# A list-scheduled decoder trunk: the planner's two rules outside the mix stage only, MLP blocks split from the residual stream, remainders of the output product by the vector engine

## The chip, the core and the metric

The kernel runs on one core of one Trainium2 chip. The metric is the time of one execution on the device in microseconds (us). Five engines take part, each with a queue of its own: TensorE (PE, the matmuls), VectorE (DVE), ScalarE (ACT), GpSimd (POOL) and SyncE (SP, which issues the loads).

## The reference

Two layers over a residual stream h of 512 tokens by 1024 channels in float32. Each layer is three steps:

```python
h = h + W_out [ attention_heads || mlstm_heads ](RMSNorm(h) @ W_in)
h = h + relu(RMSNorm(h) @ W1)^2 @ W2
h = h + sigmoid(RMSNorm(h) @ Wg + bg) * (p[i] @ Wp)
```

The attention has 8 heads of 64, two key heads, partial rotary positions, and reads for each query 128 keys that an indexer selects (the 128 largest scores). The mLSTM has 4 heads of 128, a causal convolution of width 4 ahead of its queries and keys, a forget and an input gate, and is stabilised by running maxima. W1 widens to 4096.

## The kernel before

h is held in the chip's memory, transposed, as eight blocks h[0] to h[7] of 128 channels by 512 tokens; the names const_1 to const_8 in rows below are these blocks. Each product is made of three matmuls in a reduced format: an operand x is split into hi, its rounded copy, and lo, the remainder x - hi, and hi*hi, hi*lo and lo*hi are added up (`mm3`). So for each weight tile of 128 x 1024, SP loads raw (three buffers), ACT copies it to hi, and lo is made in one of two ways, in `weight` (around line 527): DVE subtracts hi from raw; or, with adder=True, ACT writes the negated hi into lo and a DMA that POOL issues adds raw to it (an "adder"). Activation blocks are split the same way.

The three steps of a layer l are stages 3l (mix), 3l + 1 (MLP) and 3l + 2 (the gated step). The mix makes queries, keys, gates and the attention and mLSTM heads; `out_half` (line 1172) then multiplies the heads' outputs by W_OUT, four weight tiles in each of two halves, and DVE adds each block of the product to h. The MLP begins with `prep` (line 567): for each of the eight blocks it applies the norm's gain, splits the result into hi and lo, and adds up the squares for the norm's root, a running sum on POOL. With forms (the MLP's call) it also makes, for each pair of blocks, `right_sums` (line 749): half-width differences of the two, and their hi and lo, which a later product with summed weights reads. `split_block` (line 562) splits from h with the gain inside; `split` (line 744) splits a block that has the gain already.

The order of all instructions is worked out ahead by the class `Plan` (line 127). All operations of the kernel are recorded first, each with a label. `Plan.schedule` then runs through time with a table of costs: of the operations that are ready, each engine takes the most urgent by its label's priority, and the order found is written out for each engine. `lag` is what the plan allows for between an operation and the one that depends on it, 110 ns between two of VectorE. Lines 348 to 353 make an exception for small tiles: rooms "tiny" (128 x 4 and the like) and "wide" (128 x 32). `HOP` (200 ns) is the time after which the plan takes a buffer for free once its last reader is done; after an adder it takes `ADD` (5500 ns). Lines 361 to 364 hold that rule. These are numbers for the planning alone; on the chip, semaphores hold an instruction until what it needs is there. Operations of the label "forms" come behind those of "prep" in priority. Since every instruction is issued from line 395, all rows of the profile carry L395, and the tiles' names tell them apart.

Of the kernel before, what the change touches and what calls it, by code (L numbers as in the profile page):

```python
# [43 lines left out]
W_CQ, W_UP, W_QK, W_V, W_O, W_OUT, W_FF1, W_FF2, W_PLE, W_GATE, NW = 0, 2, 4, 12, 16, 20, 28, 60, 92, 94, 102  # L44
# [82 lines left out]
class Plan:  # L127
# [122 lines left out]
    def schedule(self):  # L250
# [15 lines left out]
        events, now, done = [], 0.0, 0  # L266
# [27 lines left out]
        while done < len(ops):  # L294
            moved, relaxed = True, False
            while moved or not (events or relaxed):
                relaxed = not moved
                moved = False
                for e in self.ENGINES:
                    if busy[e]:  # L300
                        continue
                    best = None
                    for key, q in queues[e].items():
                        while q and ops[q[0][1]].start is not None:
                            heapq.heappop(q)
                        if q and (best is None or q[0] < best[0]):
                            op = ops[q[0][1]]
                            if fits(op, relaxed):
                                best = (q[0], q)
                    if best is None:  # L310
                        continue
                    op = ops[heapq.heappop(best[1])[1]]
                    op.form = next(f for f in op.forms if f[0] == e)
                    op.start = op.begin = now
                    for b in op.new:
                        live[b.name] = (b, op.label, round(now / 1000))
                        if b.room in free:
                            b.place = free[b.room].pop(0)
                        for group, (kinds, cap) in self.caps.items():
                            if b.kind in kinds:  # L320
                                held[group] += 1
                    busy[e] = True
                    order.append(op)
                    op.end = now + self.cost(op.form)
                    if e == "sync" and not now:
                        op.end += 900.0
                    if e == "tensor":
                        if now - idle[0] > 3300.0:
                            idle[1] = now + 3600.0
                        if now < idle[1]:  # L330
                            op.end += self.cost(op.form)
                        idle[0] = op.end
                    heapq.heappush(events, (op.end, 0, op.n, e))
                    moved = True
                    if relaxed:
                        break
            if not events:
                stuck = [(o.n, o.label, [b.kind for b in o.new]) for e in self.ENGINES for q in queues[e].values()
                         for _, i in q[:3] for o in (ops[i],) if o.start is None]
                self.live = live  # L340
                self.stuck = []
                raise RuntimeError(f"no place: {done} of {len(ops)} {stuck[:20]} { {k: len(v) for k, v in free.items()} } {held}")
            now, what, n, e = heapq.heappop(events)
            op = ops[n]
            if what == 0:
                busy[e] = False
                done += 1
                for b in op.before:
                    o = ops[b]
                    wait = self.lag(self.source(op), o.forms[0][0])  # L350
                    if e == o.forms[0][0] == "vector" and o.writes[0].buf.room in ("tiny", "wide"):

                        wait = 0.0
                    o.ready = max(o.ready, now + wait)
                    o.left -= 1
                    if not o.left:
                        if o.ready <= now:
                            push(o)
                        else:
                            heapq.heappush(events, (o.ready, 1, o.n, None))  # L360
                for b in {id(v.buf): v.buf for v in op.reads + op.writes}.values():
                    b.users -= 1
                    if not b.users:
                        heapq.heappush(events, (now + (self.ADD if self.source(op) == "adder" else self.HOP), 2, n, b.name))
                        self.gone[b.name] = b
            elif what == 1:
                push(op)
            else:
                b = self.gone.pop(e)
                live.pop(b.name)  # L370
                if b.room in free:
                    free[b.room].append(b.place)
                for group, (kinds, cap) in self.caps.items():
                    if b.kind in kinds:
                        held[group] -= 1
# [31 lines left out]
class Trunk:  # L407
# [159 lines left out]
    def prep(self, l, gcol, forms=None):  # L567


        nc = self.nc  # L570
        label = nc.label
        cf = self.cf[l][0]
        xs, acc, last = [], None, None
        for k in range(KD):
            nc.label, nc.bias = ("prep", 0) if nc.stage else ("start", -STEP * k)
            hi, lo = self.slot([128, S], F32R), self.slot([128, S], F32R)
            if forms is None:
                self.split_block(self.h[k], cf[:, gcol + k:gcol + k + 1], hi, lo)
            else:
                x = self.slot([128, S])  # L580
                nc.scalar.activation(x, self.h[k], AF.Copy, scale=cf[:, gcol + k:gcol + k + 1])
                self.split(x, hi, lo)
                if k % 2:
                    nc.label = "forms"
                    forms.append(self.right_sums(last, x))
                last = x
            nc.bias = 0
            xs.append((hi, lo))
            nc.label = "squares" if nc.stage else "squares0"
            sq = self.slot([128, S])  # L590
            nc.scalar.activation(sq, self.h[k], AF.Square)
            if acc is None:
                acc = sq
            else:
                nacc = self.slot([128, S])
                nc.gpsimd.tensor_tensor(nacc, acc, sq, op=ALU.add)
                acc = nacc
        nc.label = label
        return xs, acc
# [571 lines left out]
    def out_half(self, l, half, cat):  # L1171

        nc = self.nc
        nc.label = nc.chain = f"out{half}"
        for n in range(KD):
            if n % 2 == 0:
                w = self.wtile(l, W_OUT + 4 * half + n // 2, adder=True)
            ps = self.psum("proj")
            for k, x in enumerate(cat):
                c = slice((n % 2) * 512 + k * 128, (n % 2) * 512 + k * 128 + 128)  # L1180
# [251 lines left out]
```

## Time and profile before

| | before |
|---|---|
| median of 3 runs | 1351.81 us (1351.55 to 1352.09) |
| the profiled execution | 1351.06 us |
| its span, first to last instruction | 1349.4 us |
| TensorE busy | 1308.7 us (97%), 7376 matmuls |
| VectorE busy | 1013.8 us (75%) |
| ScalarE busy | 738.7 us (55%) |
| GpSimd busy | 152.6 us (11%), 177 instructions |
| mean granted TensorE clock | 0.995 |

The page of the profile gives, for one execution, each engine's busy time and its share of the span. The granted clock is a share of full speed: 1.00 is 2.4 GHz, 0.50 is 1.2 GHz. In rows of a timeline the first number is the start, the second the time from there to the end of the group, then engine, line, operation and tiles, and in brackets how long the engine was idle before, and what ended that. Matmuls are pipelined, so the next begins before the last ends.

### The profile page before, as it was taken

How to read it: one execution, taken by the hardware profiler on the slowest of the kernel's cores; microseconds unless marked ns; L12 is line 12 of the kernel's file. 1: busy time of each engine (PE TensorE's matmuls, PEld its weight loads, DVE VectorE, ACT ScalarE, POOL GpSimd, SP SyncE). 2: the span in 40 equal slices, each digit the busy share in tenths (PEclk: the TensorE clock that was granted, in tenths of full speed). 3: DMA queues.
4: the chain of work that ended last, by engine and by line, in shares of the span. 5: the costliest groups of instructions: out<-in, count | busy, mean ns of one | idle time of the engine just before them, and what ended most of it. 6: DMA issues, size and time to landing. Idle time of an engine off the chain costs nothing.

```text
span 1349.4 us, 19900 instructions
## 1 busy us (share of the span) xinstructions
PE 1308.7 (97%) x7376; PEld 1124.4 (83%) x7376; DVE 1013.8 (75%) x2111; ACT 738.7 (55%) x1414; POOL 152.6 (11%) x177
## 2 busy tenths in 40 slices
PE   6999989999999999999999999899999999999998
PEld 5777878878899898988887778888789998899887
DVE  8799887488777767674858998766887777767645
ACT  4797575565444434355448957656744434434542
POOL 4132110220000000003113211003100000000120
PEclk8999999999999999999999999999999999999999
DMA  5447730653333332335235576126433333332442
GB/s 192 110 109 183 164 86 23 141 125 110 94 110 96 95 122 80 110 125 126 83 104 119 138 161 141 48 48 158 126 102 100 95 109 108 96 109 83 133 116 75
DMA packets 43874, 150.15 MB, mean 111 GB/s; under 512 B 5248, under 2 KB 5760, under 8 KB 43776
## 3 DMA queue, kind: packets, MB, share of 16 engines
q1 hardware_dynamic: 34848, 116.37, 27.5%
q0 software_dynamic: 8928, 32.51, 13.2%
q8 instruction: 58, 0.95, 0.3%
q14 instruction: 40, 0.33, 0.1%
HBM read 114.25 MB, written 2.10 MB: 86 GB/s over the span
## 4 chain that ended last, share of the span: by engine, by line
PE 79%; DVE 12%; ACT 3%; issue 3%; DMA 2%; POOL 0%; SPq 0%; DVEq 0%; ACTq 0%; POOLq 0%
PE ps_proj L395 70%; DVE s L395 4%; PE ps_sc L395 4%; PE ps_tr L395 3%; DVE tiny L395 3%; PE ps_po L395 1%; ACT s L395 1%; DVE lo L395 1%; PE ps_pn L395 1%; DMA raw<-ws 1%; DVE wide L395 1%; ACT hi L395 1%; DVE const L395 1%; DVE at L395 0%; DMA raw<-wa 0%
## 5 line engine op out<-in xcount | busy, mean ns | idle before, releaser
L395 PE MATMUL ps_proj<-s,hi 128*128 128x512 f32 (+1 forms) x3184 | 850.1, 356 | 5.4 <-DVE s L395 5.0
L395 PEld LDWEIGHTS ps_proj<-s,hi 128*128 128x128 f32 x3184 | 558.1, 189 | 92.8 <-DVE s L395 7.1
L395 PE MATMUL ps_proj<-s,lo 128*128 128x512 f32 (+1 forms) x1592 | 561.9, 355 | 1.3 <-DVE lo L395 1.3
L395 ACT ACTIVATE hi<-raw 128x1024 fp32r<-128x1024 f32 (+1 forms) x212 | 222.2, 1051 | 295.7 <-PE ps_proj L395 265.7
L395 PEld LDWEIGHTS ps_proj<-s,lo 128*128 128x128 f32 x1592 | 300.8, 189 | 46.0 <-DVE lo L395 2.9
L395 DVE TENSOR_TENSOR lo<-raw,hi 128x1024 fp32r<-128x1024 f32 (+1 forms) x149 | 184.5, 1239 | 74.4 <-ACT hi L395 74.2
L395 DVE TENSOR_TENSOR const<-const,ps_proj 128x512 f32<-128x512 f32 x160 | 109.6, 686 | 99.0 <-PE ps_proj L395 98.9
L395 POOL TENSOR_TENSOR s<-s,s 128x512 f32<-128x512 f32 x42 | 63.3, 1507 | 493.7 <-ACT s L395 481.8
L395 PE MATMUL ps_proj<-hi,s 128*128 128x512 f32 (+1 forms) x384 | 110.2, 376 | 8.4 <-ACT hi L395 7.5
L395 ACT ACTIVATE s<-s 128x512 fp32r<-128x512 f32 (+2 forms) x154 | 87.6, 619 | 15.1 <-DVE s L395 10.2
L395 POOL DMA_DIRECT2D lo<-raw x62 | 53.9, 869 | 352.4 <-ACT lo L395 275.3
L395 DVE TENSOR_TENSOR s<-s,s 128x512 fp32r<-128x512 f32 (+2 forms) x124 | 85.6, 733 | 9.3 <-ACT s L395 9.2
L395 PE MATMUL ps_sc<-s,s 128*128 128x256 f32 (+3 forms) x288 | 82.5, 373 | 3.2 <-DVE tiny L395 1.8
L395 PEld LDWEIGHTS ps_proj<-hi,s 128*128 128x128 f32 x384 | 68.5, 190 | 18.4 <-ACT hi L395 7.5
L395 ACT ACTIVATE lo<-raw 128x1024 fp32r<-128x1024 f32 x62 | 65.8, 1062 | 10.3 <-PE ps_proj L395 6.9
L395 PE MATMUL ps_proj<-lo,s 128*128 128x512 f32 (+1 forms) x192 | 65.2, 378 | 2.1 <-DVE lo L395 2.1
L395 PEld LDWEIGHTS ps_sc<-s,s 128*128 128x128 f32 x288 | 51.0, 190 | 13.0 <-issue 2.6
L395 ACT ACTIVATE s<-ps_proj 128x256 f32<-128x256 f32 (+1 forms) x104 | 42.6, 419 | 32.7 <-PE ps_proj L395 32.5
L395 ACT ACTIVATE s<-ps_tr 128x128 fp32r<-128x128 f32 (+2 forms) x174 | 42.6, 319 | 29.0 <-PE ps_tr L395 28.6
L395 ACT ACTIVATE hi<-at 128x1024 fp32r<-128x1024 f32 x28 | 29.7, 1061 | 48.0 <-PE ps_proj L395 47.7
L395 DVE TENSOR_TENSOR s<-s,ps_proj 128x256 f32<-128x256 f32 x84 | 35.2, 419 | 26.7 <-PE ps_proj L395 23.3
L395 DVE MATCH_REPLACE8 s<-m,s 128x384 f32<-128x384 f32 (+2 forms) x96 | 51.3, 539 | 0.0
(150 smaller groups left out, 1569.7 us busy)
## 6 DMA issues: line engine op xcount, KB each, us to landing
raw<-ws SPq DMA_DIRECT2D x204, 512.0 KB, 3.6
lo<-raw POOLq DMA_DIRECT2D x62, 512.0 KB, 5.3
raw<-wa SPq DMA_DIRECT2D x8, 336.0 KB, 3.6
const<-xt SPq DMA_DIRECT2D x8, 256.0 KB, 4.5
s<-pt SPq DMA_DIRECT2D x8, 256.0 KB, 3.9
out<-const SPq DMA_DIRECT2D x7, 256.0 KB, 2.0
const<-ct SPq DMA_DIRECT2D x2, 132.0 KB, 3.4
out<-const SPq DMA_DIRECT2D x2, 128.0 KB, 1.7
```

What stands on the lines that cost most here:

```text
L395: ins = getattr(getattr(nc, e), method)(*[value(x) for x in args], **{k: value(x) for k, x in kw.items()}).ins
```

## The change

It has four parts.

1. In the plan, a VectorE operation that depends on another VectorE operation was ready at once if the later one writes a tile in room "tiny" or "wide". Now this holds for "tiny" alone, and not in the mix stages (stage % 3 is 0 there). In the mix the plan lets 110 ns pass and puts other ready operations between.
2. In the mix, buffers that an adder was the last to read count as free after 200 ns in place of 5500.
3. In the MLP's `prep`, hi and lo come straight from h (`split_block`), and the block with its gain, which only the forms read, is made afterwards under the label "forms".
4. `out_half` takes the remainders of its weights by VectorE's subtraction; 16 tiles, 8 in each layer. 16 ScalarE copies and 16 DMA issues of GpSimd fall away, 16 VectorE subtractions come.

```diff
@@ -348,7 +348,7 @@
                 for b in op.before:
                     o = ops[b]
                     wait = self.lag(self.source(op), o.forms[0][0])
-                    if e == o.forms[0][0] == "vector" and o.writes[0].buf.room in ("tiny", "wide"):
+                    if e == o.forms[0][0] == "vector" and o.writes[0].buf.room == "tiny" and o.stage % 3:
 
                         wait = 0.0
                     o.ready = max(o.ready, now + wait)
@@ -361,7 +361,7 @@
                 for b in {id(v.buf): v.buf for v in op.reads + op.writes}.values():
                     b.users -= 1
                     if not b.users:
-                        heapq.heappush(events, (now + (self.ADD if self.source(op) == "adder" else self.HOP), 2, n, b.name))
+                        heapq.heappush(events, (now + (self.ADD if self.source(op) == "adder" and op.stage % 3 else self.HOP), 2, n, b.name))
                         self.gone[b.name] = b
             elif what == 1:
                 push(op)
@@ -574,14 +574,12 @@
         for k in range(KD):
             nc.label, nc.bias = ("prep", 0) if nc.stage else ("start", -STEP * k)
             hi, lo = self.slot([128, S], F32R), self.slot([128, S], F32R)
-            if forms is None:
-                self.split_block(self.h[k], cf[:, gcol + k:gcol + k + 1], hi, lo)
-            else:
+            self.split_block(self.h[k], cf[:, gcol + k:gcol + k + 1], hi, lo)
+            if forms is not None:
+                nc.label = "forms"
                 x = self.slot([128, S])
                 nc.scalar.activation(x, self.h[k], AF.Copy, scale=cf[:, gcol + k:gcol + k + 1])
-                self.split(x, hi, lo)
                 if k % 2:
-                    nc.label = "forms"
                     forms.append(self.right_sums(last, x))
                 last = x
             nc.bias = 0
@@ -1174,7 +1172,7 @@
         nc.label = nc.chain = f"out{half}"
         for n in range(KD):
             if n % 2 == 0:
-                w = self.wtile(l, W_OUT + 4 * half + n // 2, adder=True)
+                w = self.wtile(l, W_OUT + 4 * half + n // 2)
             ps = self.psum("proj")
             for k, x in enumerate(cat):
                 c = slice((n % 2) * 512 + k * 128, (n % 2) * 512 + k * 128 + 128)
```

TensorE's order is the same in the MLP and gated stages; in the mix stages 599 of 1230 matmuls stand at another place in layer 0, and 570 in layer 1. On VectorE 386 of 560 and 358 of 518 instructions of the mix moved, some 22 in an MLP stage. On SyncE's queue four of 45 and four of 32 loads moved in the mix. Five copies of attention weights (s_et) go from VectorE to ScalarE, four of them in layer 0. GpSimd issues 46 adders in place of 62.

The first place is the start of the MLP in layer 0, on VectorE. const_6 to const_8 are h[5] to h[7], an operation on one of them and ps_proj is the add of the output product; s_824 is the remainder of h[5], s_835 that of h[6] and s_819 that of h[4]; s_813, s_815, s_826, s_827, s_842 are forms. Before:

```order
L395 TENSOR_TENSOR const_6_134<-const_6_134,ps_proj_781_3170 128x512
L395 TENSOR_TENSOR s_813_3216<-s_810_3136,s_812_3201 128x512
L395 TENSOR_TENSOR s_819_3223<-s_820_3194,s_818_3209 128x512
L395 TENSOR_TENSOR s_815_3232<-s_811_3183,s_814_3214 128x512
L395 TENSOR_TENSOR const_7_161<-const_7_161,ps_proj_785_3203 128x512
L395 TENSOR_TENSOR s_826_3205<-s_825_3227,s_826_3205 128x256
L395 TENSOR_TENSOR s_827_3248<-s_825_3227,s_820_3194 128x256
L395 TENSOR_TENSOR s_827_3248<-s_825_3227,s_826_3205 128x256
L395 TENSOR_TENSOR s_824_3258<-s_825_3227,s_823_3245 128x512
L395 TENSOR_TENSOR s_842_3271<-s_836_3261 128x256
L395 TENSOR_TENSOR const_8_183<-const_8_183,ps_proj_786_3235 128x512
```

Now:

```order
L395 TENSOR_TENSOR const_6_134<-const_6_134,ps_proj_781_3165 128x512
L395 SCALAR_TENSOR_TENSOR s_819_3205<-const_5_126,const_17_87,s_818_3196 128x512
L395 TENSOR_TENSOR s_826_3213<-s_820_3203 128x256
L395 TENSOR_TENSOR const_7_161<-const_7_161,ps_proj_785_3192 128x512
L395 SCALAR_TENSOR_TENSOR s_824_3232<-const_6_134,const_17_87,s_823_3216 128x512
L395 TENSOR_TENSOR s_826_3213<-s_825_3224,s_826_3213 128x256
L395 TENSOR_TENSOR s_813_3244<-s_810_3141,s_812_3230 128x512
L395 TENSOR_TENSOR s_827_3253<-s_825_3224,s_820_3203 128x256
L395 SCALAR_TENSOR_TENSOR s_835_3257<-const_7_161,const_17_87,s_834_3241 128x512
L395 TENSOR_TENSOR const_8_183<-const_8_183,ps_proj_786_3222 128x512
```

The remainders s_824 and s_835 moved ahead of forms; s_835 now stands ahead of h[7]'s add.

The second place is the start of the kernel, on VectorE: wide_29 to wide_38 make the rotary table, lo_75 and lo_78 are remainders of the first query weights. Before:

```order
L395 TENSOR_SCALAR wide_29_265<-const_26_260 128x4 x8
L395 TENSOR_SCALAR wide_30_277<-wide_29_265 128x32
L395 TENSOR_SCALAR wide_30_277<-wide_30_277 128x32
L395 SCALAR_TENSOR_TENSOR wide_31_282<-wide_30_277,wide_29_265 128x32
L395 SCALAR_TENSOR_TENSOR wide_32_284<-wide_30_277,wide_31_282 128x32
L395 SCALAR_TENSOR_TENSOR wide_33_287<-wide_30_277,wide_32_284 128x32
L395 SCALAR_TENSOR_TENSOR wide_34_294<-wide_30_277,wide_33_287 128x32
L395 TENSOR_TENSOR lo_75_297<-raw_73_196,hi_74_263 128x1024
```

Now:

```order
L395 TENSOR_SCALAR wide_29_265<-const_26_260 128x4 x6
L395 TENSOR_TENSOR lo_75_283<-raw_73_196,hi_74_263 128x1024
L395 TENSOR_SCALAR wide_29_265<-const_26_260 128x4 x2
L395 TENSOR_SCALAR wide_30_305<-wide_29_265 128x32
L395 TENSOR_SCALAR wide_30_305<-wide_30_305 128x32
L395 TENSOR_TENSOR lo_78_309<-raw_76_230,hi_77_291 128x1024
L395 TENSOR_SCALAR tiny_82_317<-ps_tr_81_303 128x4
L395 SCALAR_TENSOR_TENSOR wide_31_320<-wide_30_305,wide_29_265 128x32
```

Both remainders moved ahead of the table's chain, and the chain is now taken apart by steps of the norm (tiny_82).

The third place is the last mLSTM head of layer 0, on VectorE. tiny_729 to tiny_742 are one chain of 16 dependent steps; ISA s_e, COPY s_et, s_577 and the like belong to the attention. Before, the 16 stand one behind the other:

```order
L395 TENSOR_TENSOR tiny_729_2702<-tiny_731_2686,tiny_371_960 128x4
L395 RECIPROCAL tiny_736_2704<-tiny_729_2702 128x4
L395 TENSOR_TENSOR tiny_737_2706<-tiny_736_2704 128x4
L395 SCALAR_TENSOR_TENSOR tiny_738_2711<-tiny_730_2682,tiny_737_2706 128x4
L395 TENSOR_SCALAR tiny_738_2711<-tiny_738_2711 128x4
L395 TENSOR_SCALAR tiny_739_2714<-tiny_738_2711 128x4
```

Now, of the same chain:

```order
L395 TENSOR_TENSOR tiny_729_2712<-tiny_731_2693,tiny_371_968 128x4
L395 RECIPROCAL tiny_736_2715<-tiny_729_2712 128x4
L395 COPY s_et_588_2718<-ps_tr_587_2665 128x512
L395 TENSOR_TENSOR tiny_737_2725<-tiny_736_2715 128x4
L395 SCALAR_TENSOR_TENSOR s_716_2727<-ps_tr_714_2700,const_20_108,s_715_2710 128x512
L395 SCALAR_TENSOR_TENSOR tiny_738_2734<-tiny_730_2689,tiny_737_2725 128x4
L395 ISA s_e_598_2737,tiny_578_2538<-ps_sc_597_2673,s_299_1859 128x512
L395 ISA tiny_578_2538 128x1
L395 TENSOR_SCALAR tiny_738_2734<-tiny_738_2734 128x4
L395 ISA s_e_602_2745,tiny_578_2538<-ps_sc_601_2731,s_299_1859 128x512
L395 ISA tiny_578_2538 128x1
L395 TENSOR_SCALAR tiny_739_2753<-tiny_738_2734 128x4
```

Of the chain's steps most have an operation of the attention, of the convolution or of another chain between them now.

## Rows read from the trace of the kernel before

**Rows 1.** The page: span, and busy time of TensorE.

```profile
span 1349.4 us, 19900 instructions
...
PE 1308.7 (97%) x7376; PEld 1124.4 (83%) x7376; DVE 1013.8 (75%) x2111; ACT 738.7 (55%) x1414; POOL 152.6 (11%) x177
```

**Rows 2.** Windows: stretch, length, each engine's busy us (instructions), clock, DMA share, GB/s.

```profile
277.35:280.83 3.48, 3.48 (x17) 2.81 (x15) 3.48 (x6) 2.69 (x5) 1.52 (x2) 1.00 0.39 134
...
172.00:231.00 59.00, 54.02 (x418) 49.38 (x416) 49.55 (x188) 41.63 (x145) 3.02 (x8) 1.00 0.17 42
...
280.83:287.46 6.63, 4.42 (x12) 2.96 (x11) 6.63 (x10) 5.18 (x9) 3.16 (x3) 0.74 0.07 19
945.96:952.97 7.01, 4.86 (x13) 3.23 (x12) 7.01 (x11) 5.52 (x10) 3.19 (x3) 0.76 0.16 34
24.84:31.20 6.36, 6.01 (x13) 4.03 (x14) 5.88 (x31) 0.00 (x0) 0.00 (x0) 0.50 0.54 169
...
30.00:45.00 15.00, 15.00 (x79) 13.37 (x79) 7.49 (x36) 7.08 (x10) 1.00 (x1) 0.95 0.17 46
...
235.00:264.00 29.00, 29.00 (x129) 23.61 (x127) 9.36 (x15) 13.65 (x17) 4.42 (x6) 1.00 0.58 127
```

**Rows 3.** Timeline of TensorE, start of the MLP, layer 0.

```profile
282.24 0.50 PE L395 MATMUL ps_proj<-s,hi 128*128 128x512 f32 x1 [1.03 <-DVE s L395]
```

**Rows 4.** Timelines of VectorE and GpSimd, the same stretch.

```profile
275.30 0.68 DVE L395 TENSOR_TENSOR const<-const,ps_proj 128x512 f32<-128x512 f32 x1
...
277.10 1.78 DVE L395 TENSOR_TENSOR s<-s,s 128x512 fp32r<-128x512 f32 x1
278.81 0.68 DVE L395 TENSOR_TENSOR const<-const,ps_proj 128x512 f32<-128x512 f32 x1
...
276.77 1.56 POOL L395 TENSOR_TENSOR s<-s,s 128x512 f32<-128x512 f32 x1 [1.68 <-issue]
```

**Rows 5.** Timelines of VectorE, ScalarE and TensorE, start of the kernel.

```profile
21.65 0.67 DVE L395 TENSOR_SCALAR wide<-const 128x4 f32<-128x4 f32 x8
...
23.57 1.22 DVE L395 TENSOR_TENSOR lo<-raw,hi 128x1024 fp32r<-128x1024 f32 x1
...
22.09 1.06 ACT L395 ACTIVATE hi<-raw 128x1024 fp32r<-128x1024 f32 x1 [4.26 <-DMA raw<-ws]
...
24.84 0.79 PE L395 MATMUL ps_proj<-s,lo 128*128 128x512 f32 x1 [0.91 <-DVE lo L395]
...
26.84 0.80 PE L395 MATMUL ps_proj<-s,lo 128*128 128x512 f32 x1 [0.35 <-DVE lo L395]
```

**Rows 6.** Timelines of SyncE, VectorE and TensorE, behind the start of the MLP, layer 0.

```profile
290.31 0.33 SPq L395 DMA_DIRECT2D raw<-ws  x1
...
295.61 0.69 DVE L395 TENSOR_TENSOR at<-raw 128x512 f32<-128x512 f32 x1 [0.91 <-DMA raw<-ws]
...
309.39 0.42 DVE L395 TENSOR_TENSOR s<-s,ps_proj 128x256 f32<-128x256 f32 x1
...
309.86 0.51 PE L395 MATMUL ps_proj<-s,hi 128*128 128x256 f32 x2 [0.40 <-DVE s L395]
```

**Rows 7.** Timelines of VectorE and TensorE, tail of mix, layer 0; tile s_et (ns min/median/max).

```profile
216.29 0.17 DVE L395 TENSOR_TENSOR tiny<-tiny,tiny 128x4 f32<-128x4 f32 x1 [2.19 <-ACT tiny L395]
...
219.28 0.16 DVE L395 TENSOR_TENSOR tiny<-tiny,tiny 128x4 f32<-128x4 f32 x1
...
220.40 0.30 PE L395 MATMUL ps_tr<-const,s_hn 128*128 128x128 f32 x1 [1.55 <-DVE s_hn L395]
...
L395 DVE COPY s_et<-ps_tr x34: 244/425/692, 182.0 to 891.1; 128x512 f32<-128x512 f32 x10, 128x128 f32<-128x128 f32 x9, 128x256 f32<-128x256 f32 x9, 128x384 f32<-128x384 f32 x6
```

**Rows 8.** The page: remainders by VectorE, and the adders' DMA (us to landing).

```profile
L395 DVE TENSOR_TENSOR lo<-raw,hi 128x1024 fp32r<-128x1024 f32 (+1 forms) x149 | 184.5, 1239 | 74.4 <-ACT hi L395 74.2
...
lo<-raw POOLq DMA_DIRECT2D x62, 512.0 KB, 5.3
```

## The prediction

> **What bounds the kernel now.** I read the page first, then the windows view, then TensorE's waits in the timeline and, for each, the work of the engine that ended it. The page [rows 1] shows TensorE (PE) busy 1308.7 us of a span of 1349.4, 97%: the kernel is bound by its matmuls, and no instruction of PE is added or removed here. What any other engine can give back is the 40.7 us in which PE idles, and the time that PE loses by running at half clock. The profiled execution took 1351.06 us: the span and 1.66 us outside it.
>
> The windows view [rows 2] shows where the change meets that idle time. It lies in the tails of the two mix stages (172 to 231 us: 59.00 less 54.02, so 4.98 idle; I take layer 1's to be alike, 10 in all) and in the starts of the two MLP stages. In an undisturbed stretch, 277.35 to 280.83, 15 matmuls begin in 3.48 us (two more reach into it), one each 0.232 us. From 280.83 to 287.46, 11 begin in 6.63 us, which at 0.232 would take 2.55: 4.08 us are lost, 2.21 of them idle, the rest by the clock, whose mean is 0.74 there, so part of it at 1.2 GHz instead of 2.4. In layer 1 the same stretch begins 12 in 7.01 us: 2.78 wanted, 4.23 lost. At the start of the kernel, 24.84 to 31.20, the clock is 0.50 (1.2 GHz) all along.
>
> What ends the wait there is VectorE's (DVE) remainder: 1.03 us at 282.24 for that of h[5] [rows 3], the other 1.18 for that of h[6]. The reason stands in DVE's own queue [rows 4]: it adds the output product to h[5] at 275.30 and to h[6] at 278.81, and between an add and the remainder of that block stand half-width sums and remainders of the "forms", which PE needs only later. DVE does not rest (6.63 busy of 6.63, [rows 2]); the remainder of h[5] comes out just before 282.24, 6 us after its add ended.
>
> **Change 3, MLP blocks split from h.** Per layer it removes nothing from DVE and adds nothing: eight TENSOR_TENSOR remainders become eight SCALAR_TENSOR_TENSOR of the same tile, eight copies by ScalarE (ACT) move behind the split under the low priority "forms". In the new order only one forms operation stands between the add of h[6] and h[5]'s remainder, and h[6]'s remainder comes ahead of h[7]'s add. From h[5]'s add, now at 275.30, there follow h[4]'s remainder, the form, h[6]'s add and h[5]'s remainder: four steps of at most 0.68 [rows 4], of which one may be stretched to 1.78, so it is done by 278 to 279, and PE asks for it at about 281.0, where its wait now begins. Four more operations, three of them half as wide, bring h[6]'s remainder by 279.8 to 281.2; it is wanted three matmuls later, at 281.7. Both waits go, and the clock has no idle time ahead of it to fall for: 4.08 and 4.23 us are the upper bound. If the half clock stayed although the waits went, 2.2 a layer are left: the lower bound of this term before what follows.
>
> What is late next [rows 6]: DVE's forms are no less work, so DVE is full as long as before. Then one chain decides: PE waits 0.40 at 309.86 for a DVE sum at 309.39, at the end of nearly unbroken DVE work that starts at 295.61, when the first weight tile for the weight sums lands; its load was issued at 290.31 and waited for a raw buffer that an adder's DMA still read. In the new order that adder's negated copy on ACT stands ahead of the last squares; the copy of the same tile's high part, which must also be done, waits behind forms: I put the load at 288.8, 1.5 earlier. Two DVE operations of 0.69 and one remainder of 1.24 [rows 6, 8] move from behind the 295.61 operation to before it, into idle time: 2.6 more. Of these 4.1 I take 3.6, since part of DVE's gap further on stays. PE arrives 4.1 earlier, finds the sum 3.6 earlier, so the wait grows from 0.40 to about 0.85. **Term: 3.6 a layer, 7.2 in all**; bounds 2 (load not earlier, half of the moved work in the way) and 8.3.
>
> **Change 1, the zero wait no longer in mix, nor for "wide".** It costs no instruction; it moves DVE's. At the kernel's start [rows 5] the remainder lo_75 stood behind the rope table's chain (23.57), now it follows six of the eight wide operations that begin at 21.65, at 0.07 to 0.08 each: 22.1 to 23.3. Then two of these and two dependent ones of about 0.2 and lo_78: about 23.85 to 25.07. Its high part was ready at 23.15 (ACT, 22.09 and 1.06), so nothing else holds it. PE, which waited 0.91 for lo_75 until 24.84 and 0.35 for lo_78 until 26.84, passes both by 25.1. **Term: 1.7 us.** From 30 to 45 us PE waits for nothing [rows 2], so it is kept. Bounds: 0.9, if lo_78 comes no earlier than it does now by more than lo_75's wait, and 3.9, if the half clock of the stretch behind it shrank too.
>
> In the mLSTM tails the tiny chains of four heads are spread between attention operations. A chain of 16 dependent steps took 3.15 us, 216.29 to 219.44, 0.20 a step, and the transposes behind it made PE wait 1.55 [rows 7]. Unshared steps cost 0.07 (the eight wide ones), so each step that something stands behind gives DVE some 0.12 us; about 41 such pairs per layer give 4.9 us.
>
> **Change 4, W_OUT remainders by DVE.** 16 ACT copies and 16 DMA issues by GpSimd (POOL) go, ACT and POOL having room; 16 DVE subtractions of 1.24 us [rows 8] come, 8 a layer, 9.9 us. The four of the second half fall in the stretch 235 to 264, where PE is never idle and DVE busy for 9.36 us of 29 [rows 2]. The four of the first half, 5.0 us, fall in the mix where DVE is nearly full: the 4.9 us from the spread chains pays for them. A raw buffer is then free after 1.24 instead of some 5.3 us of adder DMA [rows 8], which helps the loads behind on SP's queue. Five attention copies (0.43 median, [rows 7]) move from DVE to ACT, four of them in layer 0: 1.7 us less on DVE there. Against them each chain is longer, by what stands between its steps. **Term for the tails: 1.0 in layer 0 and 0.5 in layer 1**, bounds all of the idle time, 10, and a loss (rival C).
>
> What the Trainium skill says under SBUF — State Buffer, "Who interferes with whom", speaks against this part: a vector instruction with both inputs in SBUF contends with a GpSimd instruction that reads SBUF, and the later of the two waits until the other is done. The trace agrees for the MLP start, where a remainder beside GpSimd's square sum took 1.78 us and an add from PSUM 0.68 [rows 4]; the adder had no vector instruction to be held. By that rule the last subtraction of each layer, beside the first square sums, would cost 1.1 more, and the sum would come out 2.2 higher if none of it were hidden.
>
> **Change 2, buffers freed at once after adders in mix.** The plan now thinks a raw buffer free 5.3 us sooner than it is, so a load may stand in SP's queue before its buffer is free. The semaphores still hold it, and SP's order changes by four rows; I cost it at nothing, hidden by what lies in the other two raw buffers. Without that cover an ACT copy would wait for a raw tile, up to 5.3 us, with ACT's later work queued behind it.
>
> **Sum.** 1351.06 - 7.2 - 1.7 - 1.5 = 1340.7 for a profiled execution. The median of the runs, 1351.81, is 0.75 above it: 1341.4.
>
> **Rivals.**
> A, larger gain. The tails' waits vanish as well, and the half clock of the start: 10 instead of 1.5, or 3.9 instead of 1.7, on top 8.3 for 7.2: 1330 to 1339. For it: DVE has 9.4 us idle in 172 to 231 [rows 2]. Against: PE's tail waits come from several engines in turn. Chance 0.15.
> B, smaller gain. The load's earlier issue does not come, or the chain behind 295.61 was bound by something else, so that the wait at 309.86 takes the place of those removed: 2 a layer at most, and the tails give nothing: 1351.8 - 4 - 1.7 = 1346, to 1349. For it: the chain is unbroken DVE work with only 0.40 us wait at its end, so it is nearly critical now. Chance 0.20.
> C, slower. The spread chains are the critical path: between the 16 steps of the last head stand ten attention operations of 0.24 to 0.69 (by the copies, [rows 7]), some 6.2 us, and the output product's first half needs this head. If PE has nothing else to do in that time, each layer's tail grows by up to 6.2: 1351.8 - 8.9 + 12.4 = 1355.3. It decides from 4.5 us a layer on, where it eats the 8.9. For it: PE already waits 1.55 for this chain, and DVE gets four remainders more. Against: what stands between the steps was DVE's work behind them before, and PE waits for that too. Chance 0.11.
> D, nothing: the same mechanism at 4 us a layer, or B and a lost tail together: 1349 to 1354. Chance 0.09.
>
> **How the numbers follow.** My forecast, 1339 to 1345, has 0.45. Two runs of this kernel can be told apart from about 0.2%, 2.7 us. Faster: 0.45 + 0.15 + 0.20 = 0.80; same, D, 0.09; slower, C, 0.11. The range leaves out rival C, most of D and the far end of A: 1333 to 1350.
>
> **What would show it.** In the changed profile: no PE wait for DVE s between 276 and 284, and a mean clock of 1.00 there; a wait of 0.4 to 1.5 some 4 us before 309.86 less what was gained earlier; PE past lo_78 by 25.2; PE idle in each mix tail no more than 4.5; DVE's TENSOR_TENSOR remainders at 165 and POOL's adders at 46. It is wrong if the MLP start still shows clock under 0.9, if PE's idle time in a mix tail grows by over 2 us, or if ACT waits for a raw tile in the mix.

## Result, and the profile after

The changed kernel takes 1332.59 us (median of four, 1330.87 to 1333.79) against 1351.94, a ratio of 0.9854 (95% interval 0.9838 to 0.9869): 19.4 us less, where 10.4 were forecast, and 0.4 us below the range, whose lower end, 1333, lies among the four runs. Page and windows of the changed kernel, its stretches chosen to hold the same work as [rows 2], and the tail of layer 1 in the kernel before under them:

```profile
span 1330.5 us, 19866 instructions
...
PE 1305.7 (98%) x7376; PEld 1124.3 (85%) x7376; DVE 1016.6 (76%) x2122; ACT 725.2 (55%) x1403; POOL 141.5 (11%) x161
...
166.00:225.00 59.00, 58.82 (x444) 52.92 (x443) 53.08 (x201) 45.24 (x158) 2.53 (x7) 1.00 0.09 29
811.50:880.40 68.90, 68.90 (x500) 62.02 (x498) 63.22 (x218) 49.93 (x163) 3.05 (x7) 1.00 0.12 38
252.00:290.00 38.00, 38.00 (x170) 30.91 (x169) 34.15 (x59) 30.13 (x49) 13.00 (x10) 1.00 0.48 125
```

```profile
821.60:896.80 75.20, 70.42 (x497) 62.16 (x495) 61.19 (x211) 52.50 (x164) 5.20 (x10) 1.00 0.29 71
```

TensorE (PE) idles 24.8 us in place of 40.7. The tail of layer 0 idles 0.18 us where it idled 4.98 [rows 2], that of layer 1 nothing where it idled 4.78; the MLP start (252 to 290) is without a gap, its clock 1.00. Since PE runs the same matmuls, the start of the same matmul in both traces tells where the time went (us, worked out from the timelines; the last column is what the stretch up to there gave):

| first matmul of | before | changed | difference | of this stretch |
|---|---|---|---|---|
| convolution, layer 0 | 124.59 | 123.60 | -0.99 | -0.99 front of mix |
| MLP, layer 0 | 277.35 | 271.40 | -5.95 | -4.96 tail |
| gated step, layer 0 | 633.79 | 624.72 | -9.07 | -3.12 MLP |
| convolution, layer 1 | 788.92 | 778.75 | -10.17 | -1.10 gated step and front |
| MLP, layer 1 | 942.48 | 925.75 | -16.73 | -6.56 tail |
| gated step, layer 1 | 1298.37 | 1279.40 | -18.97 | -2.24 MLP |

So the tails gave 11.5 us where the prediction had 1.5, the MLP stages 5.4 where it had 7.2, the fronts (the second with the gated step before it) 2.1 where it had 1.7. In layer 1, 1.8 of the 6.56 is no idle time: by PE's timelines it changes 116 times between matmuls of the products (`ps_proj`) and the small ones of the heads in this stretch before, and 36 times now, and the non-idle part of the stretch went from 148.8 to 147.0 us. The timeline of PE in the changed kernel shows the larger waits that are left: one in the front of the mix, and one 29 us behind the first matmul of each MLP, the successor of the 0.40 of [rows 6].

```profile
98.75 0.45 PE L395 MATMUL ps_tr<-const,s_sp 128*128 128x128 f32 x3 [2.22 <-ACT vx L395]
...
300.58 0.50 PE L395 MATMUL ps_proj<-s,hi 128*128 128x256 f32 x2 [1.11 <-DVE s L395]
...
954.98 0.39 PE L395 MATMUL ps_proj<-s,hi 128*128 128x256 f32 x1 [1.21 <-DVE s L395]
```

What the tails' waits were can be read in the kernel before. PE waits seven times more like the 1.55 us of [rows 7], and these eight waits are 9.77 us, all of its idle time in both tails. Timeline of PE before:

```profile
179.56 0.73 PE L395 MATMUL ps_sc<-s,s 128*128 128x128 f32 x4 [0.93 <-DVE tiny L395]
189.01 0.44 PE L395 MATMUL ps_tr<-const,s_e 128*128 128x128 f32 x2 [1.14 <-DVE tiny L395]
197.42 0.33 PE L395 MATMUL ps_tr<-const,s_e 128*128 128x128 f32 x1 [1.36 <-DVE s L395]
...
858.58 0.50 PE L395 MATMUL ps_sc<-s,s 128*128 128x512 f32 x1 [0.86 <-DVE tiny L395]
867.74 0.33 PE L395 MATMUL ps_tr<-const,s_hn 128*128 128x128 f32 x1 [1.16 <-DVE s_hn L395]
875.35 0.51 PE L395 MATMUL ps_sc<-s,s 128*128 128x512 f32 x1 [1.40 <-DVE s L395]
...
895.63 0.33 PE L395 MATMUL ps_tr<-const,s_hn 128*128 128x128 f32 x1 [1.37 <-DVE s_hn L395]
```

There are eight mLSTM heads in the two layers. For each, VectorE (DVE) has a run of 13 or 16 tiny steps with nothing between them, and these runs end at 179.30, 188.62, 196.70, 219.44, 858.05, 866.82, 874.63 and 894.85 us: each wait ends 0.3 to 1.0 us behind one of them. The chain that [rows 7] show unbroken, in DVE's timeline of the changed kernel:

```profile
213.54 0.17 DVE L395 TENSOR_TENSOR tiny<-tiny,tiny 128x4 f32<-128x4 f32 x1 [1.92 <-ACT tiny L395]
213.74 0.18 DVE L395 RECIPROCAL tiny<-tiny 128x4 f32<-128x4 f32 x1
213.84 0.66 DVE L395 COPY s_et<-ps_tr 128x512 f32<-128x512 f32 x1
214.41 0.15 DVE L395 TENSOR_TENSOR tiny<-tiny 128x4 f32<-128x4 f32 x1
214.49 0.74 DVE L395 SCALAR_TENSOR_TENSOR s<-ps_tr,const,s 128x512 fp32r<-128x512 f32 x1
...
221.46 0.16 DVE L395 TENSOR_TENSOR tiny<-tiny,tiny 128x4 f32<-128x4 f32 x1
```

It now lasts 8.1 us (213.54 to 221.62) in place of 3.15, and PE waits for it no more: the attention's copies (s_et) and masked scores (s_e), for which PE waited while chains held DVE, go between. The freed time is near the forecast: from start to next start on DVE, the 64 steps of 128x4 of layer 0's four chains took 12.0 us in 172 to 231 before, and take 7.4 in 166 to 225 now.

### The profile page after: what moved, and what is told of

It reads as the page before. It is cut to its first block, busy times and chain, and to the rows that moved or that the text cites. A ratio compares the mean times of both kernels' runs of the same rounds, so it can differ in the third digit from the quotient of the medians.

```text
span 1330.5 us, 19866 instructions
## 1 busy us (share of the span) xinstructions
PE 1305.7 (98%) x7376; PEld 1124.3 (85%) x7376; DVE 1016.6 (76%) x2122; ACT 725.2 (55%) x1403; POOL 141.5 (11%) x161
## 5 line engine op out<-in xcount | busy, mean ns | idle before, releaser
L395 DVE TENSOR_TENSOR lo<-raw,hi 128x1024 fp32r<-128x1024 f32 (+1 forms) x165 | 202.9, 1230 | 83.9 <-ACT hi L395 76.3
L395 ACT ACTIVATE s<-s 128x512 fp32r<-128x512 f32 (+2 forms) x138 | 78.2, 620 | 13.8 <-DVE s L395 9.2
L395 PE MATMUL ps_sc<-s,s 128*128 128x512 f32 (+3 forms) x288 | 84.3, 375 | 0.6 <-ACT s_idx L395 0.2
L395 DVE TENSOR_TENSOR s<-s,s 128x512 fp32r<-128x512 f32 (+2 forms) x108 | 68.1, 667 | 9.0 <-ACT s L395 9.0
L395 POOL DMA_DIRECT2D lo<-raw x46 | 40.2, 873 | 295.8 <-ACT lo L395 237.3
L395 ACT ACTIVATE s<-const,const 128x512 fp32r<-128x512 f32 x64 | 44.2, 713 | 35.0 <-DVE const L395 35.0
L395 DVE SCALAR_TENSOR_TENSOR s<-const,const,s 128x512 fp32r<-128x512 f32 x48 | 48.0, 1009 | 17.0 <-ACT s L395 17.0
L395 ACT ACTIVATE lo<-raw 128x1024 fp32r<-128x1024 f32 x46 | 48.8, 1062 | 9.7 <-PE ps_proj L395 6.0
```

What stands on the lines that cost most here:

```text
L395: ins = getattr(getattr(nc, e), method)(*[value(x) for x in args], **{k: value(x) for k, x in kw.items()}).ins
```

## The experiments

Ratios are to the kernel before, on the same chip. What a stage gains or loses is read between the matmuls of the table above, from one profiled execution of each kernel, against the changed kernel where nothing else is said. The changed kernel profiled a second time (changed_again) agrees with the first to 0.02 us in the tails and 0.33 us in the other stages, apart from the front of the first mix, where the two lie 1.3 us apart.

**One part taken back.** The edits put the lines of before back at one place each:

```diff
undo_rule1
-  ... o.writes[0].buf.room == "tiny" and o.stage % 3:
+  ... o.writes[0].buf.room in ("tiny", "wide"):
undo_rule2
-  self.ADD if self.source(op) == "adder" and op.stage % 3 else self.HOP
+  self.ADD if self.source(op) == "adder" else self.HOP
undo_prep
   the MLP's branch of prep as before
undo_out
-  w = self.wtile(l, W_OUT + 4 * half + n // 2)
+  w = self.wtile(l, W_OUT + 4 * half + n // 2, adder=True)
```

undo_rule1. 

> The change without its first part: the zero wait holds again for tiny and wide tiles, in all stages. Theory R (the spread chains empty the tails): the idle time of TensorE in the mix tails comes back, 4 to 5 us in layer 0 and 5 to 6.6 in layer 1, and the start loses its 1 us: 1342 to 1345. Theory W (the output product's remainders by the vector engine, with the adders' copies gone from ScalarE, empty the tails): the tails stay as they are in the changed kernel, and only the start is lost: 1333 to 1335. Theory S (any new order of the list scheduler moves the tails by some us, no part is the cause): one tail returns, the other does not, 1336 to 1341.

Measured: 0.9987 (0.9975 to 0.9999), 1351.51 us. The tails are 8.1 and 8.5 us longer than in the changed kernel, the MLP stages the same to 0.7. Theory W falls, R holds, with a size above its own. The four remainders that DVE has to take in a tail do not explain that size: PE idles 5.9 and 4.4 us in the two stretches, where it idled 5.0 and 4.8 before. Beside that, the clock is 0.98 in both tails (layer 0's window stands further down) where it was 1.00 before.

undo_rule2. 

> The change without its second part: buffers count as free 5500 ns after an adder in the mix too. In the changed kernel ScalarE waited 1.75 us for a raw tile in layer 0's mix (at 97.07 us) and TensorE 2.22 behind it (at 98.75). Theory: that wait is what rule 2 costs; without the rule it goes, 2 to 3.7 us, the rest stays: 1329 to 1331. Rival: the raw tile is late whatever the plan believes, because the adder's DMA holds it, or the tails' gain hangs on rule 2's order: 1333 to 1340.

Measured: 0.9885 (0.9871 to 0.9900), 1336.89 us. The theory fell. The wait is there without the rule as well:

```profile
97.23 0.45 PE L395 MATMUL ps_tr<-const,s_sp 128*128 128x128 f32 x3 [2.24 <-ACT vx L395]
```

What is lost lies in the tails, 3.3 and 2.4 us; 1.5 and 1.1 of it is idle time of PE. The rule is no wait but an order: with it PE's matmuls of the last convolution block of layer 0 end at 182.7, without it at 208.1. That block alone is not the cause, since in half1 (below) it ends at 206.5 and the tail is 0.6 us longer; which part of the new order counts was not isolated.

undo_prep. 

> The change without its third part: the MLP's blocks get their gain first, and are split after. Theory: the two MLP starts lose what they gained net, 3.1 and 2.3 us, TensorE waits twice for VectorE at each start, 0.9 to 1.2 us each, and the half clock returns: 1336 to 1340. Rival (the later wait, 1.11 and 1.21 us behind the start, takes most of it whatever the start does): 1333 to 1335.

Measured: 0.9942 (0.9926 to 0.9958), 1344.01 us. The half of the expectation on the start held (one wait of 2.31 us there, in place of two), but the MLP stages lost 8.0 and 6.9 us, not 3.1 and 2.3: the wait behind the start grew as well, to 4.00 and 2.46. The fourth part without the third is thus 4.8 and 4.6 us slower in the MLP stages than the kernel before.

undo_out. 

> The change without its fourth part: W_OUT's remainders by adders again. Theory R (the spread chains empty the tails, DVE pays for the four remainders of a tail with what the spread gives): the tails stay within 1 us of the changed kernel's: 1331 to 1334. Theory W: TensorE's idle time in the tails comes back, 5 us in layer 0 and 6 in layer 1: 1342 to 1345.

Measured: 0.9955 (0.9940 to 0.9970), 1346.33 us. Neither held. The tails lost 0.6 and 1.7 us only, nearly as R has it, but the MLP stages, of which nobody had spoken, lost 6.3 and 7.0. Timelines of GpSimd (POOL), SyncE, DVE and PE in this run:

```profile
280.55 0.88 POOL L395 DMA_DIRECT2D lo<-raw  x1 [2.80 <-ACT lo L395]
...
285.19 0.33 SPq L395 DMA_DIRECT2D raw<-ws  x1
...
289.63 0.69 DVE L395 TENSOR_TENSOR at<-raw 128x512 f32<-128x512 f32 x1 [1.96 <-DMA raw<-ws]
...
304.69 0.58 PE L395 MATMUL ps_proj<-s,hi 128*128 128x256 f32 x1 [3.80 <-DVE s L395]
```

and the same steps in the changed kernel:

```profile
275.10 0.88 POOL L395 DMA_DIRECT2D lo<-raw  x1 [2.03 <-ACT lo L395]
...
282.11 0.33 SPq L395 DMA_DIRECT2D raw<-ws  x1
...
287.00 0.68 DVE L395 TENSOR_TENSOR at<-raw 128x512 f32<-128x512 f32 x1
```

With PE at the same place, the third W1 tile's adder goes out 5.5 us later, so its raw buffer is free and the first load of the weight sums issued 3.1 us later, and the wait is 2.7 us longer: the chain of [rows 6]. That the buffer is what the load waits for shows in the landings: here the adder lands at 285.14 and the load is issued at 285.19, in only_prep at 293.39 and 293.45. In the changed kernel the adder lands at 279.64, 2.5 us before the load. The rest of the 6.3 us are smaller waits (0.48, 0.53 and 0.63) and the clock, which is 0.89 from 304 to 320 in this run and 1.00 from 300 to 316 in the changed kernel.

**One part alone, on the kernel before.** Each is the opposite edit.

only_rule1. 

> The kernel before with the change's first part alone. Theory R (the spread chains alone empty the tails): TensorE idles less than 1 us in each mix tail, 9 to 13 us in all are gained, the MLP starts wait as before: a ratio to before of 0.990 to 0.993. Rival (the tails empty only together with the output product's remainders on the vector engine, which free ScalarE): less than half of it, 0.996 to 1.0.

Measured: 0.9954 (0.9939 to 0.9969). Between the two. Layer 0's tail gave 2.0 us; layer 1's lost 1.9, where its last mLSTM head comes behind all attention:

```profile
892.10 0.45 PE L395 MATMUL ps_tr<-const,s_hn 128*128 128x128 f32 x1 [2.87 <-DVE s_hn L395]
```

This is rival C of the prediction, in one layer and at less than its price.

only_prep. 

> The kernel before with the change's third part alone. By the prediction's step (each MLP start gains 4.1 and keeps 3.6): ratio 0.995. Theory H (the adders of the output product hold raw buffers, so that the first load of the weight sums is late, and the wait behind the start takes what the start gains): the two waits at a start go, but the wait behind it grows from 0.40 to 3 or 4 us, and the ratio is 0.998 to 1.0.

Measured: 1.0041 (1.0026 to 1.0056), slower. Each start is 2.9 and 3.1 us shorter, and then PE waits 4.26 where it waited 0.40; the MLP stages end 3.1 and 2.9 us longer than before. H holds, and more than takes the gain. Timelines of POOL, SyncE and PE:

```profile
288.79 0.87 POOL L395 DMA_DIRECT2D lo<-raw  x1 [2.80 <-ACT lo L395]
...
293.45 0.33 SPq L395 DMA_DIRECT2D raw<-ws  x1
...
313.31 0.39 PE L395 MATMUL ps_proj<-s,hi 128*128 128x256 f32 x1 [4.26 <-DVE s L395]
```

The load that was issued at 290.31 [rows 6] is issued at 293.45; the MLP of this run begins 1.7 later, so the part alone moves it 1.4 later, not 1.5 earlier, behind an adder that waited for ScalarE's (ACT) negated copy.

**Which chains, and which half of the product.**

```diff
spread_rest
-  ... == "tiny" and o.stage % 3:
+  ... == "tiny" and (o.stage % 3 or o.label == "mlstm"):
half1
-  w = self.wtile(l, W_OUT + 4 * half + n // 2)
+  w = self.wtile(l, W_OUT + 4 * half + n // 2, adder=not half)
blocks_half1
   before, with the changed prep and the line of half1
rules_only
   before, with the two changed rules
```

spread_rest. 

> The changed kernel, in which the zero wait holds again for the mLSTM heads' tiny chains in the mix, and for these alone; norm, queries and gates stay spread. Theory R (it is the mLSTM chains of 16 steps that held the vector engine while TensorE waited in the tails): the tails' idle time comes back, 8 us in each layer as without the first part: 1348 to 1351 where the changed kernel has 1332.6. Rival (the order elsewhere in the mix brings the gain): 1332 to 1338.

Measured: 0.9943 (0.9922 to 0.9965), 1345.82 us. Both tails return, 9.8 and 9.3 us, in a profiled execution that was among the long ones (span 1347.4). The median is 13.3 us above that of forms_10, a kernel as fast as the changed one, on the same chip. Windows from the first attention matmul to the output product in layer 0, of spread_rest and of undo_rule1:

```profile
156.20:236.00 79.80, 73.30 (x498) 64.94 (x497) 68.47 (x219) 49.17 (x163) 3.64 (x7) 0.96 0.10 33
```

```profile
157.30:235.50 78.20, 72.35 (x500) 64.01 (x499) 68.50 (x219) 49.11 (x163) 3.89 (x7) 0.98 0.12 35
```

PE idles 6.5 and 5.9 us in them: it is the mLSTM chains that bring the waits back, not those of norm, queries or gates. By the ratios undoing the whole rule costs some 18 us and this 13; the rest was not assigned.

half1. 

> The changed kernel, in which only the second half of the output product has its remainders by the vector engine, the first half by adders again. Theory H (the second half's adders held raw buffers and the DMA queue into the MLP start, and that is the whole gain of the fourth part): the MLP stages are as in the changed kernel, with a wait of about 1.1 us behind each start: within 2 us of it. Rival (the first half in the mix tail matters, or both): the tails or the MLP stages lose 3 us or more, in all 5 to 13 us, as without the fourth part.

Measured: 0.9853 (0.9837 to 0.9870), 1333.26 us against 1331.48 of the changed kernel on the same chip. The MLP stages are those of the changed kernel to 0.1 us, the wait behind the start is 0.95 and 1.57, the tails are 0.6 and 1.6 us longer. H holds: the fourth part's gain lies in the second half, whose adders' DMAs ran into the MLP.

blocks_half1. 

> The kernel before with the third part, and with the vector engine's remainders for the second half of the output product alone; both planning rules as before. Theory H (part three loses alone because the second half's adders hold up the W1 tiles behind them; with these gone it gains): each MLP stage 2.3 to 3.0 us shorter than before, the tails as before: a ratio of 0.995 to 0.997. Rival (the MLP gain hangs on the tails or the rules): 0.999 to 1.004, as the third part alone.

Measured: 0.9936 (0.9923 to 0.9948), somewhat more than expected. The MLP stages are 3.0 and 3.1 us shorter than before, the tails as before, and the wait behind the start is 1.42. The same third part that costs 3 us a layer alone brings 3 us with the second half's adders gone.

rules_only. 

> The kernel before with the two planning rules alone. Theory R2 (rule 1 alone let the last mLSTM head of layer 1 come last, with a wait of 2.87 us for it, because the plan held raw buffers for 5.5 us after adders and so ran the convolution late; rule 2 lets the convolution's blocks come earlier): both tails empty, the MLP starts wait as before: 0.990 to 0.992. Rival (the remainders by the vector engine bring layer 1's order): as rule 1 alone, 0.994 to 0.997.

Measured: 0.9885 (0.9869 to 0.9901), a little more than expected. Tails 4.4 and 5.0 us shorter; windows of layer 1's tail, and PE's waits in the MLP start, which are still there:

```profile
814.70:883.30 68.60, 68.60 (x496) 61.60 (x494) 58.29 (x205) 50.24 (x161) 4.97 (x11) 1.00 0.29 69
...
276.48 0.50 PE L395 MATMUL ps_proj<-s,hi 128*128 128x512 f32 x1 [0.93 <-DVE s L395]
278.61 0.50 PE L395 MATMUL ps_proj<-s,hi 128*128 128x512 f32 x1 [1.18 <-DVE s L395]
```

So R2 holds for the two rules alone: in layer 1 the first loses 1.9 us, and both together gain 5.0. The rival is not out, though: in undo_rule2, without rule 2 but with the third and fourth parts, layer 1's tail is 4.1 us shorter than before. Rule 2 or those parts, either gives the first rule most of its gain there. Together with blocks_half1 (spans 11.4 and 5.8 us below 1349.4) this makes 17.2 of the 18.9.

**The waits that are left, and a faster version.**

```diff
forms_10
-  "forms": 40
+  "forms": 10
gate_sum   (first pair of each MLP: the last remainder is made behind the sum; so is the next pair's first)
+  if later:
+      self.gate = len(nc.ops) - 1
+      later()
+      nc.ops[-1].after[self.gate] = True
...
gate_vx    (layer 0, last tile of W_O: the adder's copy behind three vx copies)
+  for v in range(first, first + 3):
+      nc.ops[-2].after[v] = True
```

forms_10. 

> The changed kernel with the label forms at priority 10 in place of 40, so that ScalarE's copies of the first W1 tiles stand ahead of the last forms. In the changed kernel the load of the first tile of the weight sums was issued at 282.11, held by the copy hi<-raw that stood behind two forms, and TensorE waited 1.11 and 1.21 us some 18 us later. Theory: the load is issued by 280 or before, the two waits go, ratio to before 0.983 to 0.985. Rival (the vector engine's own work between the load and the wait is the bound): the load is earlier, the waits stay, 0.985 to 0.987.

Measured: 0.9837 (0.9821 to 0.9853), 1332.56 us: by ratio, which lies where the theory had it, it cannot be told from the changed kernel. The rival holds by the waits, which stay, 1.61 and 1.98 us, though the load comes 10 us earlier. Timelines of SyncE, DVE and PE:

```profile
272.09 0.33 SPq L395 DMA_DIRECT2D raw<-ws  x1
...
275.71 0.72 DVE L395 TENSOR_TENSOR at<-raw 128x512 f32<-128x512 f32 x1 [1.55 <-DMA raw<-ws]
...
299.68 0.51 PE L395 MATMUL ps_proj<-s,hi 128*128 128x256 f32 x2 [1.61 <-DVE s L395]
```

changed_again. 

> The changed kernel once more, beside the three that are built on it. Its ratio to before should come out within 0.983 to 0.987 again; the other three are read against it.

Measured: 0.9846 (0.9832 to 0.9861), 1331.48 us.

gate_sum. 

> The changed kernel, in which the first pair of W1 blocks makes its last remainder (1.22 us of the vector engine) after the sum that reads TensorE's bank, not before it. TensorE waited 1.11 and 1.21 us in the two MLP stages until that sum was done. Theory: the vector engine's order in this place is the bound, both waits go: 1.0 to 2.3 us below the changed kernel, a ratio of 0.9983 to 0.9993 to it. Rival (the sum itself waits for something that comes at the same time): no change.

Measured: 0.9838 (0.9823 to 0.9852), 1330.35 us, 1.1 below the changed kernel (a ratio of 0.9992). The waits shrank from 1.42 and 1.13 (changed_again) to 0.84 and 0.53, they did not go: DVE's order in this place is a part of the bound.

gate_vx. 

> The changed kernel, in which ScalarE's copy for the last adder of the output gate's weights, in layer 0, stands behind three of the four vx copies, not ahead of them. TensorE waited 2.22 us for the first vx copy, which stood behind that copy, which waited 1.75 for its load. Theory: the wait goes and 1 to 2.2 us are kept. Rival (the loads behind are late by then, whatever ScalarE does first, and set TensorE's pace up to 124 us): the wait goes or moves, and nothing is kept by the start of the convolution.

Measured: 0.9822 (0.9803 to 0.9841), 1327.97 us (1326.00 to 1331.37), 3.5 below changed_again. The wait of 2.2 is gone, and PE reaches the convolution 4.0 us earlier than the start of the queries would give. More than the wait is won, since the half clock behind it is gone too; windows of the changed kernel and of gate_vx:

```profile
96.00:106.00 10.00, 7.73 (x31) 5.75 (x29) 10.00 (x34) 7.56 (x14) 2.77 (x4) 0.83 0.91 225
```

```profile
96.00:106.00 10.00, 10.00 (x46) 8.03 (x47) 10.00 (x33) 8.31 (x18) 4.15 (x7) 1.00 0.99 233
```

By the MLP 2.6 of the 4.0 are lost again in this execution, most at a new wait for DVE, which gate_both, with the same order of PE in the mix, does not show:

```profile
164.75 0.59 PE L395 MATMUL ps_sc<-s,s 128*128 128x384 f32 x1 [1.81 <-DVE s_t L395]
```

gate_both. 

> The changed kernel with both moves, the first pair's last remainder behind the sum and the adder's copy behind three vx copies. Theory: they lie 200 us apart and add: 0.981 to 0.983 to before, 3 to 4.5 us below the changed kernel. Rival (what the first gives is taken by the next wait): as one of them, 0.982 to 0.984.

Measured: 0.9808 (0.9790 to 0.9826), the lowest ratio, median 1329.03 us where before had 1353.70 on that chip; its five runs go from 1323.98 to 1330.33. In the profiled execution (1323.98) PE keeps all 4.0 us up to the MLP, and the wait behind the start is 0.59. That it beats the changed kernel rests on ratios from two chips, 0.9808 and 0.9846, whose intervals just do not meet; how much of it each move brings was not settled.

## Why the prediction was wrong, point by point

**The direction was right, and three of its steps.** PE is the bound, and the gain is for the most part idle time and half clock given back. The two waits of each MLP start went and the clock there is 1.00: 4.06 us in layer 0 up to the norm's first matmul, forecast 4.1. The spread chains freed 4.7 us of DVE in the tail, forecast 4.9. TENSOR_TENSOR remainders of weights are 165, adders 46.

**The term that failed is "Term for the tails: 1.0 in layer 0 and 0.5 in layer 1".** It measured 5.0 and 6.6. The step was to set the time freed on DVE against the four remainders that come to it, and the longer chains against PE. Both are busy-time sums of a stage that was bound by order: while a chain ran unbroken, the small operations that PE needed stood behind it. Against the larger gain the prediction held that "PE's tail waits come from several engines in turn"; the rows of the kernel before say otherwise, all eight come behind a chain of DVE. The chain became 5 us longer at no cost, and the four remainders did not lengthen the tails: with adders in their place these are 0.6 and 1.6 us longer (half1). spread_rest shows that it is the mLSTM chains. Rule 2, "I cost it at nothing", is worth 3.3 and 2.4 us a tail in the changed kernel, and in layer 1 rule 1 lost by itself (only_rule1): a figure for planning alone changes which block comes first. The larger part of rival A, which had 0.15, is what happened: the tails' waits vanished. The clock from 24.84 to 31.20 is 0.73 in place of 0.50 [rows 2], but the 3.9 and the 8.3 of that rival did not come. The sign "if ACT waits for a raw tile in the mix" did show, 1.75 us at 97.07 (below), but not by rule 2: undo_rule2 has the wait of PE behind it as well.

**The MLP term, 7.2, measured 5.4.** The follow-on wait was named and sized 0.85; it is 1.11 and 1.21, and DVE's own order there is a part of its bound (forms_10, gate_sum). The reason given for the term was wrong: the third part was credited with the earlier load. Alone it has the load later and is slower (only_prep); the earlier load comes only with the second half of the product on DVE, which the prediction noted as "helps the loads behind" and priced at nothing. blocks_half1 shows the two together at 3.0 and 3.1. That the term came out near its forecast is luck: it needed the fourth part, which the prediction had put into another term. With the planner's two rules in place, the MLP stages differ from those before by (us):

| | layer 0 | layer 1 |
|---|---|---|
| the rules alone (rules_only) | +0.1 | +0.6 |
| with the third part (undo_out) | +3.2 | +4.8 |
| with the fourth part (undo_prep) | +4.8 | +4.6 |
| with both (the changed kernel) | -3.1 | -2.2 |

**The start, 1.7.** PE passed lo_78 at 25.00, forecast 25.1, and began the queries 2.4 us earlier. By the convolution 0.99 is left: the wait for vx (98.75) took most of the rest, and gate_vx gave it back. Both figures are of one execution. In eleven profiled executions of kernels with rule 1 (those with gate_vx's move aside) the convolution begins at 122.06 to 123.72, in the four of kernels without it at 124.59 to 124.81: 0.9 to 2.8 us, around the 1.7 of the forecast. The sentence that it "is kept" looked at PE's waits up to 45 us only; the next thing that was late lay at 97, a load issued at 91.23, for which an adder's copy waited with the vx copies behind it. Timelines of ACT and SyncE:

```profile
97.07 1.06 ACT L395 ACTIVATE lo<-raw 128x1024 fp32r<-128x1024 f32 x1 [1.75 <-DMA raw<-ws]
...
91.23 0.33 SPq L395 DMA_DIRECT2D raw<-ws  x1
```

**Contention of DVE and GpSimd** changed no term: a remainder still took 1.78 us beside a square sum in the changed kernel (277.02), and PE did not wait for it. The 1.1 a layer that the prediction weighed against the fourth part did not come: the last subtraction of W_OUT took 1.22 us in each layer (255.51 and 909.85), as the others.

## What to carry to other kernels

A planner that lets dependent small steps follow at once makes a chain that nothing enters; if another engine waits for work queued behind it, spread the chain, even if it then ends later, and look that nothing comes to wait for its end, as in layer 1 of only_rule1. When a change removes a wait, price it up to the next wait of the same engine, and ask which buffer that one hangs on: two parts, each slower in a stage without the other, can make that stage faster together. Before a gain is priced by busy time, list every wait of the bounding engine and see what the engine that ended it had been doing.

## What the runs showed of the hardware that was not expected

The adders' DMAs, 512 KB each, land later where other transfers are in flight. Of the 46 in the changed kernel, the nine with no load and no other adder between issue and landing took 4.5 to 5.1 us, the 13 with one or more beside them on average 5.0 to 8.2, with a median of 6.2. In the kernel before the two ranges are 4.5 to 5.2 and 4.8 to 7.5. The view of the tile lo on GpSimd, changed kernel:

```profile
DMA to landing us min/median/max: 4.5/5.1/8.2
```

And the start's half clock is not the kernel's alone: the changed kernel, profiled twice (the second is changed_again), had a mean clock of 0.89 and of 1.00 from 24.84 to 40 us, and its queries began 1.2 us apart. Windows of both:

```profile
24.84:40.00 15.16, 15.00 (x68) 12.75 (x68) 8.34 (x51) 4.53 (x7) 0.00 (x0) 0.89 0.24 75
```

```profile
24.84:40.00 15.16, 14.87 (x76) 12.72 (x77) 9.39 (x55) 5.70 (x9) 0.70 (x1) 1.00 0.31 100
```
